# Attention operands of a hybrid layer turned by transposing transfers instead of on TensorE

## The chip, the cores and the metric

The kernel runs on one core of a Trainium2 chip. The metric is the device time of one execution in microseconds; below, "median" is the median of three runs. PE is TensorE, PEld its weight loads, DVE VectorE, ACT ScalarE, POOL GpSimd, SP SyncE. Transfers are issued from SP, POOL or ACT and run on the core's 16 DMA engines.

## What is computed

One decoder layer on 256 tokens of width 2048, in float32: a half-step SwiGLU feed-forward (width 5632), a mixer (chunked spatial gating beside a Mamba-2 scan) between one input and one output projection, cross attention of 4 heads of 512 into 256 memory tokens, a second half-step feed-forward, a final norm. The change touches the attention:

```python
def memory_cross_attention(hn, memn, w_q, w_kv, w_o):
    q = (hn @ w_q).reshape(bn, s, XA_HEADS, XA_HEADDIM)
    k, v = jnp.split(memn @ w_kv, 2, axis=-1)
    ...
    logits = jnp.einsum('bshd,bmhd->bhsm', q, k).astype(jnp.float32) * (XA_HEADDIM ** -0.5)
    probs = jax.nn.softmax(logits, axis=-1).astype(v.dtype)
    o = jnp.einsum('bhsm,bmhd->bshd', probs, v).reshape(bn, s, D_MODEL)
    return o @ w_o
```

## The kernel before

Precision is kept by splitting. Each float32 operand x becomes a high part (a rounded copy, type fp32r) and a low part (x minus the high part); a product is three matmuls, high by high, high by low and low by high. Activations are split once, weights as they stream in.

**A projection** (`proj_sum`) takes the weights in eight pieces of 256 rows by two blocks of 512 columns (1 MB). A piece is loaded by SP into one of three buffers (`wraw`), its high part is cast by ACT (`high`, L169), its low part subtracted by DVE (`low` through `split_op`, L177). There are three buffers for high and two for low parts. A plain piece (kind "C") takes 24 matmuls of 512 columns. A piece with sums (kind "S") combines blocks as in Strassen's scheme: three more DVE additions and a second split, but 21 matmuls. Eight PSUM banks are in use while a projection has S pieces ahead; four of them are combined after the last S piece (`mid`, `parts_of`), the others at the end (`evac`). The attention's projections are two for queries (heads 0 and 1, then 2 and 3), two for keys, two for values, each with eight pieces of which two have sums, in fourth and sixth place.

**The order of work.** PE runs in the order in which the program is written. Work beside the weights is put off with `later(fn, by)`: `step()` is called after each piece (or half piece) and runs the jobs that are due, counted in pieces; a job that needs a PSUM bank is held back while the S pieces run, unless it is marked `bankless`. On the other engines the framework's scheduler orders instructions when the program is built, within their dependencies and within the explicit orders that `behind` adds: casts and splits of weights (`last_cast`, `last_split`) keep their order, and `in_turn` puts the casts and splits of a source named "turned" into that order too.

**Temporaries** of 2 KB per partition (`half_k`, tag "t2k") share six buffers: partial results ("part"), copies ("halves"), turned operands ("turned"), probabilities ("probs"), sums of operands ("forms").

**How operands are turned.** PE needs activations with the features on the partitions. In the two feed-forwards the hidden activations go through DRAM (`Pieces.turn_later`, L481): ACT copies each 128 x 512 block so that the upper and lower 16 bits of its numbers lie apart ("halves", L485), POOL writes them to a DRAM tile ("planes", L487), and one piece later SP reads 256 columns at a time back with a transposing transfer ("turned", L491), which works on 16-bit elements. Four pieces later ACT and DVE split the turned block (L385, L386, or L471 to L477 for an S piece).

In the attention, queries and keys are turned on PE. `by_head` (L1034) collects a head's result and calls `operand_later`, which in `to_operand` makes four PE transposes (L77) per half into a PSUM bank one piece after the projection (L385 and L386 split from there). `attend` (from two pieces after the key projection) makes the logits, 24 matmuls per head, then maximum, exponentials and scaling (L1059 to L1068). `turn_probs`, 1.5 pieces later, transposes the probabilities on PE, and they are split at L992 and L993. `weigh` multiplies them with the values one and two pieces after the value projections.

Of the kernel before, what the change touches and what calls it, by code (L numbers as in the profile page):

```python
# [17 lines left out]
P = 128  # L18
# [29 lines left out]
def hybrid_layer(ctx: ExitStack, tc: tile.TileContext, x, xt, mem, memt, w_gu1, w_dn1, w_in, w_s, w_out,  # L48
# [30 lines left out]
    def later(fn, by=1, bankless=False):  # L79
        put_off.append((steps[0] + by, len(put_off), fn, bankless))  # L80
# [12 lines left out]
    def half_k(dtype, name):  # L93
        return tmp.tile([P, NC], dtype, name=name, tag="t2k")
# [267 lines left out]
        return r  # L362


    def in_turn(src, last, op):

        if not src.tensor.name.startswith("turned"):
            return op()
        with behind(last):
            ins = op()  # L370
        last[:] = [ins.ins]
        return ins

    def to_operand(srcs, dst, q, c0=None, of=None):
        of = q if of is None else of
        if isinstance(srcs, list):
            ps = side("tpose").rearrange("p (k s) -> p k s", k=2)
            for k in range(2):
                for t in range(NT):
                    transpose(out=ps[:, k, t * P:(t + 1) * P],  # L380
                              in_=srcs[t][:, (of + k) * P:(of + k + 1) * P], identity=ident)
        else:
            ps = srcs
        if c0 is None:
            hi = in_turn(ps, last_cast, lambda: nc.scalar.copy(out=dst[:, q:q + 2, :S], in_=ps))  # L385
            lo = in_turn(ps, last_split, lambda: nc.vector.tensor_tensor(  # L386
                out=dst[:, q:q + 2, S:], in0=ps, in1=dst[:, q:q + 2, :S].bitcast(F32), op=ALU.subtract))
        else:
            scs = [col[:, c0 + of + k:c0 + of + k + 1] for k in range(2)]
            for k in range(2):  # L390
                hi = nc.scalar.activation(dst[:, q + k, :S], ps[:, k, :], AF.Copy, scale=scs[k])
            for k in range(2):
                lo = nc.vector.scalar_tensor_tensor(out=dst[:, q + k, S:], in0=ps[:, k, :], scalar=scs[k],
                                                    in1=dst[:, q + k, :S].bitcast(F32),
                                                    op0=ALU.mult, op1=ALU.subtract)
        return hi.ins, lo.ins


    def operand_later(srcs, to, name, c0=None, by=1):
        def half(q):  # L400
            if q == 0:
                to.append(slot([P, KG, 2 * S], F32R, name))
            return to_operand(srcs, to[at], q, c0)

        at = len(to) + sum(1 for o in owed if o is to)
        owed.append(to)

        def first():
            owed.remove(to)
            assert len(to) == at  # L410
            half(0)
            later(lambda: half(2), by=0)

        later(first, by)

    owed = []


    class Pieces(dict):
        def __init__(self, kinds, name, donor=None):  # L420

            self.kinds, self.name, self.half, self.made, self.donor = kinds, name, None, {}, donor

        def add(self, srcs, q, c0):

# [31 lines left out]
        def sums(self, dst, ps, c0=None):  # L457
            in_sbuf = ps.tensor.name.startswith("turned")
            if not in_sbuf or c0 is not None:
                a = half_k(F32, "forms").rearrange("p (f s) -> p f s", f=4)  # L460
            if in_sbuf and c0 is None:
                a = ps
            elif c0 is None:
                nc.scalar.copy(out=a, in_=ps)
            else:
                for k in range(2):
                    nc.scalar.activation(a[:, 2 * k:2 * k + 2], ps[:, 2 * k:2 * k + 2], AF.Copy,
                                         scale=col[:, c0 + k:c0 + k + 1])

            b = half_k(F32, "forms").rearrange("p (f s) -> p f s", f=4)  # L470
            in_turn(a, last_split, lambda: nc.vector.tensor_tensor(  # L471
                out=b[:, 0:2], in0=a[:, 1:2].broadcast_to([P, 2, P]), in1=a[:, 0:4:3], op=ALU.subtract))
            nc.vector.tensor_tensor(out=b[:, 2], in0=a[:, 0], in1=b[:, 1], op=ALU.subtract)
            nc.vector.tensor_tensor(out=b[:, 3], in0=a[:, 2], in1=b[:, 2], op=ALU.subtract)
            for x, f0, f1 in ((a, 0, 4), (b, 4, 8)):
                hi = in_turn(x, last_cast, lambda: nc.scalar.copy(out=dst[:, 0, f0:f1], in_=x))
                lo = nc.vector.tensor_tensor(out=dst[:, 1, f0:f1], in0=x, in1=dst[:, 0, f0:f1].bitcast(F32),  # L477
                                             op=ALU.subtract)
            return hi.ins, lo.ins

        def turn_later(self, srcs, by):  # L481
            planes = dram.tile([S, 2, NC], U16, name="planes", tag="planes", bufs=2)
            for t in range(NT):
                halves = tmp.tile([P, 2 * NC], U16, name="halves", tag="t2k")
                nc.scalar.copy(out=halves.rearrange("p (b n) -> p b n", b=2),  # L485
                               in_=srcs[t].bitcast(U16).rearrange("p (n b) -> p b n", b=2))
                nc.gpsimd.dma_start(out=planes[t * P:(t + 1) * P].rearrange("p b n -> p (b n)"), in_=halves)  # L487
            for q in (0, 2):
                def fetch(q=q):
                    to = half_k(F32, "turned").rearrange("p (k s) -> p k s", k=KP)  # L490
                    nc.sync.dma_start(out=to.bitcast(U16).rearrange("p k s -> p (k s)").rearrange("p (k s) -> p k s", k=KP),  # L491
                                      in_=planes[:, :, q * P:(q + 2) * P].rearrange("s b n -> (s b) n"), transpose=True)
                    later(lambda: self.put(len(self), to, 0, None), by=by[1], bankless=True)
                later(fetch, by=by[0] + q / 4, bankless=True)

        def later(self, srcs, c0=None, by=1):
            for q in (0, 2):
# [530 lines left out]
    def by_head(to, name, scale=None):  # L1028
        got = {}

        def take(j, t, x):
            got[j, t] = x
            if scale is not None:
                nc.scalar.mul(x, x, scale[:, t:t + 1])  # L1034
            if t == 1:
                operand_later([got[j, 0], got[j, 1]], to, name, by=1 + j / 2)

        return take

# [10 lines left out]
    def attend(hd, kt):  # L1050
        lg = side("logits").rearrange("p (t m) -> p t m", t=NT)
        for t in range(NT):
            for i in range(4):
                qh, ql = qts[hd][:, i, t * P:(t + 1) * P], qts[hd][:, i, S + t * P:S + (t + 1) * P]
                matmul(lg[:, t, :], qh, kt[:, i, :S], start=(i == 0), stop=False)
                matmul(lg[:, t, :], qh, kt[:, i, S:])
                matmul(lg[:, t, :], ql, kt[:, i, :S], start=False, stop=(i == 3))
        mx = small.tile([P, NT], F32, name="mx")
        nc.vector.tensor_reduce(out=mx, in_=lg, axis=AX.X, op=ALU.max)  # L1059
        nc.vector.scalar_tensor_tensor(out=mx, in0=mx, scalar=-1.0, in1=lscale, op0=ALU.mult, op1=ALU.mult)  # L1060
        pr = half_k(F32, "probs").rearrange("p (t m) -> p t m", t=NT)
        sm = small.tile([P, NT], F32, name="sm")
        for t in range(NT):
            nc.scalar.activation(pr[:, t, :], lg[:, t, :], AF.Exp, bias=mx[:, t:t + 1], scale=lscale[:, t:t + 1],
                                 accum_out=sm[:, t:t + 1])
        nc.vector.reciprocal(out=sm, in_=sm)
        for t in range(NT):
            nc.vector.tensor_scalar(out=pr[:, t, :], in0=pr[:, t, :], scalar1=sm[:, t:t + 1], scalar2=None, op0=ALU.mult)  # L1068
        later(lambda: turn_probs(hd, pr), by=1.5)

    def turn_probs(hd, pr):
        tps = side("tpose").rearrange("p (m s) -> p m s", m=2)
        for m in range(2):
            for t in range(NT):
                transpose(out=tps[:, m, t * P:(t + 1) * P], in_=pr[:, t, m * P:(m + 1) * P], identity=ident)
        if hd % 2 == 0:
            pts.append(slot([P, 2, 2, 2 * S], F32R, "pts"))
        split_to(pts[hd // 2][:, hd % 2], tps)

    for hd in (0, 2):  # L1080
        heads(w_kv, mem_ts, MEM_KINDS, MEM_ORDER, hd * XD, by_head(kts, "kt", rstd_mem))
        for j in range(2):
            later(lambda hd=hd + j: attend(hd, kts[hd]), by=2 + j / 2)

    O_KINDS = "CCCSCSCC"
    ots = Pieces(O_KINDS, "ot")
# [100 lines left out]
```

## Time and profile before

| | |
|---|---|
| three runs | 2435.13, 2433.65, 2434.24 us; median 2434.24 |
| the profiled execution | 2435.73 us, span 2433.9 us |
| DMA | 503.86 MB, mean 207 GB/s |
| ScalarE casts of weights (L169, raw) | 787.2 us, 438 instructions |
| VectorE splits of weights (L177, lo from raw) | 944.8 us, 446 instructions |

How it is read: a row of the profile gives for an engine or a group of instructions the time in which it was busy; the chain of waits follows the execution back from its last instruction, at each step to what released it. Matmuls overlap in PE, so the length of one record is more than the time that it takes from PE; that time is read from the distance between starts, or from the lengths in the chain. A transfer has an issuing time on its queue and a time to landing.

### The profile page before, as it was taken

The page shows a single profiled execution, that of the slowest core. Times are in us where ns is not written, and L with a number is a line of the kernel's source. Part 1 is how long each engine was busy: PE and PEld are TensorE (multiplying, and loading weights), DVE is VectorE, ACT ScalarE, POOL GpSimd, SP SyncE. Part 2 cuts the span into 40 slices and gives each one's busy share as a digit, 9 for nine tenths or more (in the row PEclk, how much of TensorE's full clock was granted, in tenths as well). Part 3 has the DMA queues.
Part 4 walks back from the last instruction along what each step waited for, and adds up shares of the span by engine and source line. Part 5 has one row for each costly group of instructions (what it writes and reads, how often), then busy time and mean ns, then how long its engine had stood idle before and what let it go on. Part 6 is the DMA issues. An engine that isn't in the chain of part 4 may idle for free.

```text
span 2433.9 us, 29019 instructions
## 1 busy us (share of the span) xinstructions
PE 2420.0 (99%) x11189; PEld 2015.2 (83%) x11189; DVE 2033.6 (84%) x1936; ACT 1351.3 (56%) x1248; POOL 51.3 (2%) x104
## 2 busy tenths in 40 slices
PE   9999999999999999999999999999999999999998
PEld 7888888888888888788888888888888888888887
DVE  7999889999877777655698988778899988899997
ACT  6666445656546554435555655555566554556554
POOL 0000000000000000000000000000000000000000
PEclk9999999999999999999999999999999999999999
DMA  8768667777655555545566655555567776777774
GB/s 294 230 223 242 203 198 233 223 228 231 203 185 191 183 182 190 191 163 185 187 204 226 231 188 171 173 178 180 187 217 241 225 210 205 220 227 228 232 219 154
DMA packets 252714, 503.86 MB, mean 207 GB/s; under 512 B 62864, under 2 KB 66992, under 8 KB 251808
## 3 DMA queue, kind: packets, MB, share of 16 engines
q1 hardware_dynamic: 245696, 477.95, 61.7%
q0 software_dynamic: 6048, 23.02, 2.5%
q8 instruction: 87, 1.43, 0.2%
q10 hardware_dynamic: 832, 1.05, 0.1%
q14 instruction: 51, 0.42, 0.0%
HBM read 476.76 MB, written 13.66 MB: 201 GB/s over the span
## 4 chain that ended last, share of the span: by engine, by line
PE 95%; issue 2%; DMA 1%; DVE 0%; ACT 0%; SPq 0%; POOL 0%; POOLq 0%; DVEq 0%; ACTq 0%
PE acc L74 91%; PE tpose L77 1%; DMA raw<-in_w_gu 1%; PE yp L74 1%; PE o L74 0%; PE logits L74 0%; DMA h<-in_x 0%; PE mixed L74 0%; PE dt L74 0%; DVE sum L177 0%; PE scores L74 0%; PE yo L74 0%; PE st L74 0%; ACT hi L169 0%; DVE lo L177 0%
## 5 line engine op out<-in xcount | busy, mean ns | idle before, releaser
L177 DVE TENSOR_TENSOR lo<-raw,hi 128x2048 fp32r<-128x2048 f32 (+2 forms) x446 | 944.8, 2119 | 259.1 <-PE acc L74 197.5
L169 ACT CAST hi<-raw 128x2048 fp32r<-128x2048 f32 (+1 forms) x438 | 787.2, 1798 | 515.9 <-PE acc L74 441.9
L74 PE MATMUL acc<-hi,xp_ffn 128*128 128x512 f32 x1824 | 574.6, 390 | 0.0
L74 PEld LDWEIGHTS acc<-hi,xp_ffn 128*128 128x128 f32 x1824 | 342.8, 188 | 71.2
L169 ACT CAST hi<-sum 128x2048 fp32r<-128x2048 f32 x117 | 224.1, 1915 | 294.1 <-DVE sum L177 156.5
L74 PE MATMUL acc<-lo,xp_ffn 128*128 128x512 f32 x912 | 355.3, 390 | 2.0 <-DVE lo L177 2.0
L177 DVE TENSOR_TENSOR lo<-sum,hi 128x2048 fp32r<-128x2048 f32 x117 | 268.1, 2292 | 36.7 <-ACT hi L169 36.6
L74 PE MATMUL acc<-hi,hid 128*128 128x512 f32 x896 | 281.8, 389 | 0.0
L74 PE MATMUL acc<-hi,xt_mix 128*128 128x512 f32 x768 | 242.6, 393 | 0.0
L74 PEld LDWEIGHTS acc<-lo,xp_ffn 128*128 128x128 f32 x912 | 171.3, 188 | 38.6 <-DVE lo L177 3.2
L568 DVE TENSOR_TENSOR part<-acc,part 128x512 f32<-128x512 f32 x272 | 180.7, 686 | 22.1 <-PE acc L74 8.7
L74 PEld LDWEIGHTS acc<-hi,hid 128*128 128x128 f32 x896 | 168.2, 188 | 34.9
L74 PE MATMUL acc<-lo,hid 128*128 128x512 f32 x448 | 174.3, 389 | 0.0
L74 PEld LDWEIGHTS acc<-hi,xt_mix 128*128 128x128 f32 x768 | 144.2, 188 | 30.6 <-issue 1.0
L177 DVE TENSOR_TENSOR sum<-sum,raw 128x512 f32<-128x512 f32 x234 | 161.6, 691 | 6.2
L74 PE MATMUL acc<-lo,xt_mix 128*128 128x512 f32 x384 | 149.6, 390 | 0.0
L74 PE MATMUL acc<-hi,xp_ffn1s 128*128 128x512 f32 x466 | 148.6, 389 | 0.0
L74 PE MATMUL acc<-hi,xp_ffn2s 128*128 128x512 f32 x466 | 148.5, 389 | 0.0
L177 DVE TENSOR_TENSOR sum<-raw 128x1024 f32<-128x1024 f32 x117 | 142.5, 1218 | 0.3 <-DMA raw<-in_w_gu 0.3
L74 PE MATMUL acc<-xt_mix,hi 128*128 128x512 f32 x512 | 140.5, 396 | 0.0
L74 PE MATMUL acc<-hi,hids 128*128 128x512 f32 x392 | 125.2, 389 | 0.0
L74 PE MATMUL acc<-hi,memt 128*128 128x512 f32 x384 | 123.4, 392 | 0.0
(292 smaller groups left out, 3147.7 us busy)
## 6 DMA issues: line engine op xcount, KB each, us to landing
raw<-in_w_gu SPq DMA_DIRECT2D x286, 512.0 KB, 4.6
raw<-in_w_in SPq DMA_DIRECT2D x80, 1024.0 KB, 5.1
raw<-in_w_dn SPq DMA_DIRECT2D x60, 1024.0 KB, 5.2
raw<-in_w_gu SPq DMA_DIRECT2D x132, 256.0 KB, 4.9
raw<-in_w_kv SPq DMA_DIRECT2D x24, 1024.0 KB, 5.2
raw<-in_w_out SPq DMA_DIRECT2D x21, 1024.0 KB, 5.1
raw<-in_w_dn SPq DMA_DIRECT2D x28, 512.0 KB, 4.1
raw<-in_w_dn SPq DMA_DIRECT2D x56, 256.0 KB, 4.6
```

The costliest lines, as they stand in the source:

```text
L74: return pe(nc.tensor.matmul(out, lhsT=lhsT, rhs=rhs, start=start, stop=stop))
L77: return pe(nc.tensor.transpose(out=out, in_=in_, identity=identity))
L169: last_cast[:] = [nc.scalar.copy(out=t[:, :n], in_=x[:, :n]).ins]
L177: last_split[:] = [nc.vector.tensor_tensor(**kw).ins]
L568: nc.vector.tensor_tensor(out=out, in0=a, in1=b, op=op)
```

## The change

`turn_later` is taken apart into functions that any operand can use: `write_planes` (copies and writes), `read_turned` (the transposing read) and `turn_over`. Queries and keys go through them with `operand_turned`: copies and writes at the end of the projection, reads 1 and 1.5 pieces later for the first head and 1.25 and 1.75 for the second, splits 4 pieces after each read. The probabilities are copied and written in `attend`, read one piece later and split four pieces after that, from SBUF instead of PSUM. The logits are due 7 and 7.5 pieces after the key projection instead of 2 and 2.5.

```diff
+    def write_planes(srcs, n=NC):
+        planes = dram.tile([len(srcs) * P, 2, n], U16, name="planes", tag="planes", bufs=4)
+        for t, src in enumerate(srcs):
+            halves = tmp.tile([P, 2 * n], U16, name="halves", tag="t2k")
+            nc.scalar.copy(out=halves.rearrange("p (b n) -> p b n", b=2),
+                           in_=src.bitcast(U16).rearrange("p (n b) -> p b n", b=2))
+            nc.gpsimd.dma_start(out=planes[t * P:(t + 1) * P].rearrange("p b n -> p (b n)"), in_=halves)
+        return planes
+
+    def read_turned(to, planes, c0, n):
+        nc.sync.dma_start(out=to, in_=planes[:, :, c0:c0 + n].rearrange("s b n -> (s b) n"), transpose=True)
+
+    def turn_over(srcs, by, put):
+        planes = write_planes(srcs)
+
+        def fetch(q):
+            to = half_k(F32, "turned")
+            read_turned(to.bitcast(U16).rearrange("p (k s) -> p k s", k=KP), planes, q * P, KP * P)
+            later(lambda: put(to.rearrange("p (k s) -> p k s", k=KP), q), by=by[1], bankless=True)
+
+        for q in (0, 2):
+            later(lambda q=q: fetch(q), by=by[0] + q / 4, bankless=True)
+
-    def in_turn(src, last, op):
-
-        if not src.tensor.name.startswith("turned"):
+    def in_turn(src, last, op, c0=None):
+
+        if not src.tensor.name.startswith("turned") or c0 is not None and c0 < C_MIX:
             return op()
...
+    def operand_turned(srcs, to, name, c0=None, by=(1, 4)):
+        at = len(to) + sum(1 for o in owed if o is to)
+        owed.append(to)
+
+        def put(src, q):
+            if q == 0:
+                owed.remove(to)
+                assert len(to) == at
+                to.append(slot([P, KG, 2 * S], F32R, name))
+            to_operand(src, to[at], q, c0)
+
+        turn_over(srcs, by, put)
+
...
-        def turn_later(self, srcs, by):
-            planes = dram.tile([S, 2, NC], U16, name="planes", tag="planes", bufs=2)
...
+        def turn_later(self, srcs, by, c0=None, at=None):
+            if at is None:
+                at = self.due
+                self.due += 2
+            turn_over(srcs, by, lambda to, q: self.put(at + q // 2, to, q, c0))
...
-                operand_later([got[j, 0], got[j, 1]], to, name, by=1 + j / 2)
+                operand_turned([got[j, 0], got[j, 1]], to, name, by=(1 + j / 4, 4))
...
-        later(lambda: turn_probs(hd, pr), by=1.5)
-
-    def turn_probs(hd, pr):
-        tps = side("tpose").rearrange("p (m s) -> p m s", m=2)
-        for m in range(2):
-            for t in range(NT):
-                transpose(out=tps[:, m, t * P:(t + 1) * P], in_=pr[:, t, m * P:(m + 1) * P], identity=ident)
+        planes = write_planes([pr[:, t, :] for t in range(NT)], S)
+        later(lambda: turn_probs(hd, planes), by=1, bankless=True)
+
+    def turn_probs(hd, planes):
+        to = half_k(F32, "turned")
+        read_turned(to.bitcast(U16).rearrange("p (k s) -> p k s", k=KP), planes, 0, S)
+        later(lambda: split_probs(hd, to.rearrange("p (m s) -> p m s", m=2)), by=4, bankless=True)
+
+    def split_probs(hd, tps):
         if hd % 2 == 0:
             pts.append(slot([P, 2, 2, 2 * S], F32R, "pts"))
-        split_to(pts[hd // 2][:, hd % 2], tps)
+        to_operand(tps, pts[hd // 2][:, hd % 2], 0)
...
-            later(lambda hd=hd + j: attend(hd, kts[hd]), by=2 + j / 2)
+            later(lambda hd=hd + j: attend(hd, kts[hd]), by=7 + j / 2)
```

The parts left out pass the scale's column `c0` on to `in_turn` in `to_operand` and `Pieces.sums`, so that scaled casts and splits of a turned source would keep the order as well.

More of the change, by code (lines that the diff above doesn't have):

```diff
@@ L390, in to_operand @@
             for k in range(2):
-                hi = nc.scalar.activation(dst[:, q + k, :S], ps[:, k, :], AF.Copy, scale=scs[k])
+                hi = in_turn(ps, last_cast, lambda k=k: nc.scalar.activation(
+                    dst[:, q + k, :S], ps[:, k, :], AF.Copy, scale=scs[k]), c0)
             for k in range(2):
-                lo = nc.vector.scalar_tensor_tensor(out=dst[:, q + k, S:], in0=ps[:, k, :], scalar=scs[k],
-                                                    in1=dst[:, q + k, :S].bitcast(F32),
-                                                    op0=ALU.mult, op1=ALU.subtract)
+                lo = in_turn(ps, last_split, lambda k=k: nc.vector.scalar_tensor_tensor(
+                    out=dst[:, q + k, S:], in0=ps[:, k, :], scalar=scs[k], in1=dst[:, q + k, :S].bitcast(F32),
+                    op0=ALU.mult, op1=ALU.subtract), c0)
         return hi.ins, lo.ins
@@ L422, in __init__ @@
             self.kinds, self.name, self.half, self.made, self.donor = kinds, name, None, {}, donor
+            self.due = 0
         def add(self, srcs, q, c0):
@@ L466, in sums @@
                 for k in range(2):
-                    nc.scalar.activation(a[:, 2 * k:2 * k + 2], ps[:, 2 * k:2 * k + 2], AF.Copy,
-                                         scale=col[:, c0 + k:c0 + k + 1])
+                    in_turn(ps, last_cast, lambda k=k: nc.scalar.activation(
+                        a[:, 2 * k:2 * k + 2], ps[:, 2 * k:2 * k + 2], AF.Copy, scale=col[:, c0 + k:c0 + k + 1]), c0)
             b = half_k(F32, "forms").rearrange("p (f s) -> p f s", f=4)
-            in_turn(a, last_split, lambda: nc.vector.tensor_tensor(
-                out=b[:, 0:2], in0=a[:, 1:2].broadcast_to([P, 2, P]), in1=a[:, 0:4:3], op=ALU.subtract))
+            in_turn(ps, last_split, lambda: nc.vector.tensor_tensor(
+                out=b[:, 0:2], in0=a[:, 1:2].broadcast_to([P, 2, P]), in1=a[:, 0:4:3], op=ALU.subtract), c0)
             nc.vector.tensor_tensor(out=b[:, 2], in0=a[:, 0], in1=b[:, 1], op=ALU.subtract)
@@ L479, in sums @@
             return hi.ins, lo.ins
-        def turn_later(self, srcs, by):
-            planes = dram.tile([S, 2, NC], U16, name="planes", tag="planes", bufs=2)
-            for t in range(NT):
[L484 to L494, printed above, removed]
+        def turn_later(self, srcs, by, c0=None, at=None):
[3 more added lines that the diff above has]
+            turn_over(srcs, by, lambda to, q: self.put(at + q // 2, to, q, c0))
         def later(self, srcs, c0=None, by=1):
@@ L1068, in attend @@
             nc.vector.tensor_scalar(out=pr[:, t, :], in0=pr[:, t, :], scalar1=sm[:, t:t + 1], scalar2=None, op0=ALU.mult)
-        later(lambda: turn_probs(hd, pr), by=1.5)
-    def turn_probs(hd, pr):
-        tps = side("tpose").rearrange("p (m s) -> p m s", m=2)
-        for m in range(2):
-            for t in range(NT):
-                transpose(out=tps[:, m, t * P:(t + 1) * P], in_=pr[:, t, m * P:(m + 1) * P], identity=ident)
+        planes = write_planes([pr[:, t, :] for t in range(NT)], S)
[5 more added lines that the diff above has]
+    def split_probs(hd, tps):
         if hd % 2 == 0:
             pts.append(slot([P, 2, 2, 2 * S], F32R, "pts"))
-        split_to(pts[hd // 2][:, hd % 2], tps)
+        to_operand(tps, pts[hd // 2][:, hd % 2], 0)
     for hd in (0, 2):
```

## The prediction

> **What bounds the kernel now.** I read the page first, then the chain of waits inside the attention, then a table of windows, then the feed-forward groups, where the same kind of transfer already runs.
>
> ```profile
> span 2433.9 us, 29019 instructions
> PE 2420.0 (99%) x11189; PEld 2015.2 (83%) x11189; DVE 2033.6 (84%) x1936; ACT 1351.3 (56%) x1248; POOL 51.3 (2%) x104
> PE 95%; issue 2%; DMA 1%; DVE 0%; ACT 0%; SPq 0%; POOL 0%; POOLq 0%; DVEq 0%; ACTq 0%
> ```
>
> TensorE (PE) is busy 99% of the span and carries 95% of the chain that ends last. So an instruction taken off PE is time gained, as long as nothing makes PE wait instead. The chain between 1400 and 1600 us (second query projection, both key projections, start of the value projections) has 37 pieces; these are the ones of the second query projection and the first logits:
>
> ```profile
> by line: PE acc L74 90.0%; PE logits L74 5.7%; PE tpose L77 4.4%
> ...
> 1408.99 0.44 PE tpose L77 x4
> 1409.42 2.78 PE acc L74 x12
> 1412.20 0.87 PE tpose L77 x8
> ...
> 1415.82 0.44 PE tpose L77 x4
> 1416.26 36.78 PE acc L74 x162
> ...
> 1507.12 2.87 PE logits L74 x24
> ...
> 1533.32 0.87 PE tpose L77 x8
> ```
>
> The columns are start, length, what, how many instructions. Every piece is PE: nobody else is ever late here. 162 matmuls take 36.78 us, 0.227 us each, so a plain piece of weights (24 matmuls) is 5.45 us and a piece with sums (21) 4.77 us. The windows say the same; the first four are the second query, the two key and the first value projection, the next two are feed-forward groups, the last the 3 us in which two transposing transfers run:
>
> ```profile
> core 0: us, PE busy (x) PEld busy (x) DVE busy (x) ACT busy (x) POOL busy (x), PEclk, DMA share, GB/s
> 1405.00:1450.00 45.00, 45.00 (x208) 37.32 (x207) 39.79 (x44) 26.21 (x29) 0.30 (x2) 1.00 0.60 194
> 1450.00:1497.00 47.00, 47.00 (x217) 38.82 (x216) 39.96 (x37) 27.43 (x25) 0.00 (x0) 1.00 0.60 191
> 1497.00:1548.00 51.00, 51.00 (x263) 43.39 (x262) 38.77 (x41) 28.21 (x31) 0.00 (x0) 1.00 0.50 165
> 1548.00:1595.00 47.00, 47.00 (x243) 40.00 (x241) 36.14 (x39) 24.11 (x27) 0.00 (x0) 1.00 0.51 163
> 2100.00:2143.00 43.00, 43.00 (x192) 35.60 (x190) 39.43 (x34) 25.91 (x20) 1.08 (x2) 1.00 0.77 231
> 2143.00:2186.00 43.00, 43.00 (x191) 35.63 (x190) 39.55 (x33) 25.19 (x19) 1.08 (x2) 1.00 0.74 229
> 2145.00:2148.00 3.00, 3.00 (x15) 2.45 (x15) 3.00 (x2) 1.49 (x1) 0.00 (x0) 1.00 1.16 185
> ```
>
> PE has no idle time in any of them and the clock is full. VectorE (DVE) has 40 us of work in 47 in the attention, and 39.4 in 43 in a feed-forward group. T below is the step at which a projection ends; a step is one piece.
>
> **Removed: 80 transposes on PE.**
>
> ```profile
> L77 PE MATMUL tpose<-ident,part x64: 270/272/273, 1408.8 to 1554.8; 128*128 128x128 f32 x64
> L77 PE MATMUL tpose<-ident,probs x16: 272/272/273, 1533.2 to 1584.7; 128*128 128x128 f32 x16
> ```
>
> Queries and keys have 64, in each of four projections a group of 4, one of 8, one of 4; the probabilities have 16, in two groups of 8. By the chain a 4 takes 0.44 us and an 8 takes 0.87: 8 x 0.44 + 6 x 0.87 = 8.74 us, 0.109 each. All of it lies on the path, since PE never waits there: -8.74 us.
>
> The records last 272 ns, two and a half times that, because they overlap. The Trainium skill (TensorE: Matmul & The Clock Gate, Part 4: PE-mode transpose) puts a 128x128 transpose inside a kernel at about 275 ns; by that the sum would be 80 x 275 ns = 22 us. The trace agrees with it as the length of a record, not as what the transpose takes from PE.
>
> **Added: the way through DRAM.** Per operand two copies on ScalarE (ACT), two writes from GpSimd (POOL), two transposing reads from SyncE (SP); per head of probabilities 2, 2 and 1. In all 24 copies, 24 writes, 20 reads. The feed-forward groups show them:
>
> ```profile
> L485 ACT COPY halves<-part x44: 1036/1046/1051, 59.4 to 2304.7; 128x1024 uint16<-128x1024 uint16 x44
> L487 POOL DMA_DIRECT2D planes<-halves x44: 542/542/637, 60.7 to 2306.0; - x44
> L491 SPq DMA_TRANSPOSE turned<-planes x44: 1225/1303/3480, 64.1 to 2311.8; - x44
> planes<-halves POOLq DMA_DIRECT2D x44, 256.0 KB, 4.4
> turned<-planes SPq DMA_TRANSPOSE x44, 4.1
> SPq L491 <- DMA planes<-halves: 29.2, 23, 2.4
> ```
>
> ACT: 16 x 1.05 us, and 8 copies of half the size for which there is no row, between half and all of 1.05: 21 to 25 us. The first four windows hold 106 us of ACT in 190; with 25 more it is 131, about 69%. Cost 0; were ACT full, all of it would count. POOL: 24 x 0.54 = 13 us on an engine with 0.3 us of work there. Cost 0.
>
> SP: 20 x 1.3 = 26 us, and each read waits for its writes, with the weight loads queued behind it. In a feed-forward group the wait is 1.3 us (29.2 over 23) and the two reads 2.6, so loads stand still 3.9 us; here, with two operands, up to 1.3 + 4 x 1.3 = 6.5 us at each of four ends of a projection. Loads at a feed-forward group's end stand still without any loss on PE, with DVE fuller (39.4 of 43) than here. I take 0; the other end is in the rivals.
>
> The DMA engines: in the 3 us of two reads they are full (share 1.16) and bring only 185 GB/s. The Trainium skill (DMA: Bandwidth & Descriptors, Specifications) says that transfers in pieces under 512 B fall below line rate, which speaks against this change; the trace agrees, 185 GB/s at a full share against 229 at 0.74 in the window of 43 us around it. Four reads need 6 us of the engines per projection, and the share there is 0.5 to 0.6; 6 of 47 us more is 0.13, the four writes less than that, which ends near the 0.77 of the feed-forward groups.
>
> **Changed in place: the splits.** They read SBUF, not PSUM.
>
> ```profile
> L385 ACT CAST kt<-tpose x8: 566/584/594, 1497.8 to 1555.1; 128x512 fp32r<-128x512 f32 x8
> L386 DVE TENSOR_TENSOR kt<-tpose,kt x8: 680/688/692, 1498.4 to 1556.2; 128x512 fp32r<-128x512 f32 x8
> L385 ACT CAST hid<-turned x28: 610/613/616, 74.7 to 2278.4; 128x512 fp32r<-128x512 f32 x28
> L386 DVE TENSOR_TENSOR hid<-turned,hid x28: 683/685/685, 77.9 to 2281.7; 128x512 fp32r<-128x512 f32 x28
> ```
>
> Twenty of each: ACT +0.6 us, DVE nothing. They also no longer need a PSUM bank. Cost 0.
>
> **Moved: the logits, from T+2 to T+7.** Each head's 24 matmuls (2.87 us), maximum, exponentials and scaling go past five pieces on PE, and past their splits on ACT and DVE; new behind them are the copies, writes and read of the probabilities. The work is the same. What goes is 5.7 us of PE time that stood ahead of the first piece with sums, in which DVE could catch up; the key splits and the maxima leave the same place. The second query projection has no logits ahead of its sums and shows PE 45.00 of 45.00. Cost 0. Ready keys: in a feed-forward group the way from the first copy to the last split is
>
> ```profile
> L485 ACT COPY halves<-part x2: 1039/1042/1046, 2135.6 to 2138.8; 128x1024 uint16<-128x1024 uint16 x2
> L386 DVE TENSOR_TENSOR hid<-turned,hid x2: 685/685/685, 2154.0 to 2157.3; 128x512 fp32r<-128x512 f32 x2
> ```
>
> 2158.0 - 2135.6 = 22.4 us with the same due steps for its two halves. Seven pieces, two with sums, are 5 x 5.45 + 2 x 4.77 = 36.8 us: 14 us to spare. Probabilities are split at T+12 and used at T+17. Cost 0. Queries are needed later still.
>
> **The rest of the diff** executes what stood. Only the input of the first feed-forward is both turned and scaled, its c0 is below C_MIX, and so it is still not put behind the last cast or split; the pieces of the feed-forwards get the same numbers; four buffers for the planes instead of two can only lift a wait. Cost 0.
>
> **Sum.** -8.74 us. The profiled execution took 2435.73 us, 1.83 outside its span; it would be 2427.0. The median of before is 2434.24, so I forecast 2425.5 us. 0.2%, 4.9 us, is about what a measurement of this kernel can tell from no change.
>
> **Rivals.**
> 1. Weights late. The 6.5 us in which loads stand still are not hidden by the one piece (5.45 us) that is split ahead: 1.05 us lost at each of four projections, 4.2 in all: 2429.7. Against it: the feed-forward groups, and that in the attention casts wait for PE to free a buffer and not for loads:
>
> ```profile
> ACT hi L169 <- PE acc L74: 39.2, 16, 4.2
> ```
>
> That is 2.5 us to spare for each of 16 casts. For it: twice as many reads in one place. Without any split ahead, 6.5 - 2.5 = 4.0 us each would be lost, 16 in all.
> 2. Slower: the keys come late at the logits of heads 2 and 3. The pool for temporaries has six buffers. At the end of the second key projection four hold its result, one a head's probabilities, and copies have one left. A copy holds its buffer for 1.05 + 0.54 + 4.4 = 6.0 us. If all eight copies there (four of probabilities, four of keys) go through one buffer, the way is 48 + 1.3 + 4.1 + 0.6 + 0.7 = 54.7 us against 36.8: PE waits 17.9 us, with all later matmuls behind it, and the time is 2425.5 + 17.9 = 2443.4. It decides from 8.7 us late, when more than six of the eight go one behind the other. Against it: each pair of copied results frees two buffers at once.
> 3. The record's length is the price: 80 x 272 ns = 21.8 us off, 2412.5. The chain speaks against it: eight transposes in 0.87 us. The page on TensorE above would have it so.
>
> **Chances.** Forecast 0.80, weights late 0.12, slower 0.06, record's length 0.02. Runs of before spread by 0.7 us to either side and the sum's terms are measured, so below I go to 2424.0. Above, the range takes in the weights being late with 1.3 us more: 2431.0. That leaves out 0.08 and the tails. Faster by over 0.2% (under 2429.4): 0.80 + 0.02 and the lighter part of rival 1, 0.02: 0.84. Same: 0.10. Slower: 0.06.
>
> **What would show it.** PE busy near 2411 us with 80 fewer matmuls, no tpose fed by part or probs, chain in the attention all PE. ACT up by 21 to 25 us, DVE unchanged, POOL +13, 64 transposing reads. Rival 1 would show as PE or PEld waiting for DVE lo with ACT hi waiting for a load; rival 2 as PE logits waiting for the split of kt. Wrong I would be if PE's idle time rose by 4 us or more, wherever.

## The result and the profile after

The changed kernel takes 2447.68 us (median of six runs, 2445.65 to 2451.57) against 2434.57 us for the kernel before in the same series: the ratio is 1.0055 [1.0044, 1.0065]. It is slower by 0.55%, where 2425.5 us was forecast. Two executions, one of the kernel before and one of run 2 below, ran at a much lower clock (4510.15 and 3108.87 us); they are left out of the medians and of every comparison. The profiled execution took 2448.37 us. Its page:

```profile
span 2446.7 us, 29000 instructions
PE 2419.4 (99%) x11109; PEld 2010.2 (82%) x11109; DVE 2033.2 (83%) x1936; ACT 1371.0 (56%) x1272; POOL 66.3 (3%) x128
PE 88%; issue 8%; DMA 1%; ACT 1%; DVE 1%; POOL 1%; SPq 0%; POOLq 0%; ACTq 0%; DVEq 0%
```

PE has 80 matmuls fewer, as it should, and yet is busy for as long as before (in part because the half clock found below lengthens its records); its share of the chain has fallen from 95% to 88%. The windows of the attention (second query, first key, second key, first value projection; columns as in the prediction) show where:

```profile
1405.00:1445.00 40.00, 36.90 (x161) 29.60 (x160) 32.65 (x36) 26.45 (x33) 5.13 (x6) 1.00 0.76 220
1445.00:1495.00 50.00, 45.67 (x189) 36.86 (x188) 37.99 (x38) 28.16 (x27) 2.24 (x4) 0.93 0.76 226
1495.00:1540.00 45.00, 44.34 (x203) 36.66 (x202) 35.81 (x29) 28.49 (x24) 2.17 (x4) 1.00 0.77 240
1540.00:1595.00 55.00, 47.93 (x212) 38.52 (x211) 36.57 (x40) 32.52 (x38) 4.34 (x8) 0.94 0.70 192
```

Where PE was busy for every microsecond of before, it now idles 190.00 - 174.84 = 15.2 us, and in two of the windows the granted clock (the share of its full clock that PE was given) is below 1. The waits between 1400 and 1600 us say for whom (the last row is the queue of SP's transfers):

```profile
PEld acc L74 <- DVE lo L177: 19.2, 10, 3.4
PE acc L74 <- DVE lo L177: 15.0, 9, 3.1
ACT hi L169 <- DMA raw<-in_w_kv: 6.4, 2, 3.4
ACT hi L169 <- DMA raw<-in_w_q: 4.1, 1, 4.1
ACT kt L408 <- DMA turned<-planes: 6.5, 4, 3.6
ACT halves L369 <- DMA planes<-halves: 3.0, 2, 2.1
SPq L375 <- DMA planes<-halves: 24.1, 7, 6.7
```

PE and its weight loads wait for low parts of weights. Behind that ACT waits for loads of weights, for which it had no wait in these 200 us before, for turned blocks, and for a buffer that a write still holds; and SP waits 24.1 us in seven reads for the writes to land, 3.4 us each, not the 1.3 us of a feed-forward group.

Most of it falls on one kind of piece: the second piece with sums of a projection, with 13.0 of the 15.1 us of pauses in PE's rows. The first key projection shows it best. In the kernel before, the low part of that piece's sums is ready just in time (start, length, what; the number in brackets is idle time):

```profile
1476.99 2.29 DVE L177 TENSOR_TENSOR lo<-sum,hi 128x2048 fp32r<-128x2048 f32 x1 [0.39 <-ACT hi L169]
1478.53 0.39 PE L74 MATMUL acc<-hi,memts 128*128 128x512 f32 x1
1479.34 0.19 PEld L74 LDWEIGHTS acc<-lo,memts 128*128 128x128 f32 x1 [0.17 <-DVE lo L177]
```

It ends at 1476.99 + 2.29 = 1479.28, and PEld, which had stood waiting for it for 0.17 us, takes it up at 1479.34. The wait cost PE nothing, but nothing was left to spare either. In the same way the second query projection has 0.8 us to spare there, the second key and the first value projection 1.3 us each. So "PE has no idle time" was true of before and said nothing of how near it was to having some. These are the loads on SP around that piece, before and after the change, and then what ACT, DVE and PE did after it:

```profile
1452.49 0.38 SPq L140 DMA_DIRECT2D raw<-in_w_kv  x1
1458.39 0.38 SPq L151 DMA_DIRECT2D raw<-in_w_kv  x1
```

```profile
1453.19 0.38 SPq L140 DMA_DIRECT2D raw<-in_w_kv  x1
1454.85 9.87 SPq L375 DMA_TRANSPOSE turned<-planes  x3
1464.83 0.60 SPq L151 DMA_DIRECT2D raw<-in_w_kv  x1
1465.53 1.24 SPq L375 DMA_TRANSPOSE turned<-planes  x1
1466.82 1.04 SPq L154 DMA_DIRECT2D raw<-in_w_kv  x2
```

```profile
1472.76 1.48 ACT L169 CAST hi<-raw 128x1536 fp32r<-128x1536 f32 x1 [3.40 <-DMA raw<-in_w_kv]
1477.36 0.39 PE L74 MATMUL acc<-hi,memts 128*128 128x512 f32 x1
1480.39 0.50 PE L74 MATMUL acc<-lo,memts 128*128 128x512 f32 x1 [2.65 <-DVE lo L177]
1480.69 2.29 DVE L177 TENSOR_TENSOR lo<-sum,hi 128x2048 fp32r<-128x2048 f32 x1 [0.35 <-ACT hi L169]
1483.04 0.79 PE L74 MATMUL acc<-lo,memts 128*128 128x512 f32 x1 [1.68 <-DVE lo L177]
```

L151 and L154 are the loads of the second piece with sums. In the kernel before SP issues nothing between 1452.9 and 1458.4 either, 5.5 us: there it waits until DVE has freed a buffer. Now it is 11.3 us, 1453.6 to 1464.8: three reads stand there with their waits, 9.87 us, and the fourth stands in the middle of the next load. ACT waits 3.40 us for that load, DVE's low part of the sums ends 5.6 us after PE has begun the piece (0.8 us after in the kernel before: 1479.28 and 1478.53), and PE stops twice in it, for 2.65 and 1.68 us.

Then comes something that no row of before shows:

```profile
1477.00:1483.50 6.50, 2.17 (x8) 1.23 (x7) 6.08 (x6) 4.74 (x5) 0.00 (x0) 0.88 0.29 83
1483.50:1488.50 5.00, 5.00 (x13) 3.84 (x13) 2.89 (x3) 1.76 (x1) 0.00 (x0) 0.50 0.55 177
1585.50:1591.00 5.50, 5.50 (x13) 4.33 (x14) 3.23 (x3) 2.10 (x2) 0.00 (x0) 0.50 0.60 202
```

After these pauses, and again after those of the first value projection, PE works for 5 to 6 us at half clock: the 13 matmuls of a window take 0.4 us each instead of 0.227. That is 2.5 and 2.75 us more. 15.2 us of idle time and 5.25 us of half clock make 20.4 us; the 23.0 us found below are more. Counted from start to start, the pauses take 16.9 us beyond a matmul's 0.227 us, because a record of 0.39 us covers part of each pause, and the matmuls that start over 0.33 us apart take 6.6 us beyond it: 23.5 us.

### The profile page after: what moved, and what is told of

Its sections match the earlier page's. It is cut to its first block, busy times and chain, and to the rows that moved or that the text cites. A ratio compares the mean times of both kernels' runs of the same rounds, so it can differ in the third digit from the quotient of the medians.

```text
span 2446.7 us, 29000 instructions
## 1 busy us (share of the span) xinstructions
PE 2419.4 (99%) x11109; PEld 2010.2 (82%) x11109; DVE 2033.2 (83%) x1936; ACT 1371.0 (56%) x1272; POOL 66.3 (3%) x128
## 4 chain that ended last, share of the span: by engine, by line
PE 88%; issue 8%; DMA 1%; ACT 1%; DVE 1%; POOL 1%; SPq 0%; POOLq 0%; ACTq 0%; DVEq 0%
PE acc L74 85%; PE tpose L77 1%; PE yp L74 1%; DMA raw<-in_w_gu 0%; PE o L74 0%; ACT hi L169 0%; POOL planes L371 0%; PE mixed L74 0%; DVE lo L177 0%; PE logits L74 0%; DMA turned<-planes 0%; DMA planes<-halves 0%; DVE sum L177 0%; PE dt L74 0%; PE scores L74 0%
## 5 line engine op out<-in xcount | busy, mean ns | idle before, releaser
L177 DVE TENSOR_TENSOR lo<-raw,hi 128x2048 fp32r<-128x2048 f32 (+2 forms) x446 | 944.6, 2119 | 265.6 <-PE acc L74 183.7
L177 DVE TENSOR_TENSOR lo<-sum,hi 128x2048 fp32r<-128x2048 f32 x117 | 268.1, 2291 | 41.0 <-ACT hi L169 40.8
L177 DVE TENSOR_TENSOR sum<-sum,raw 128x512 f32<-128x512 f32 x234 | 161.5, 690 | 6.3
L177 DVE TENSOR_TENSOR sum<-raw 128x1024 f32<-128x1024 f32 x117 | 142.4, 1217 | 1.6 <-DMA raw<-in_w_kv 0.7
```

The costliest lines, as they stand in the source:

```text
L177: last_split[:] = [nc.vector.tensor_tensor(**kw).ins]
```

## The experiments

Times are medians; the interval is that of the ratio to the kernel before, whose median in the four series was 2434.60 (first four runs), 2434.79 (next four), 2434.49 (two) and 2434.89 us (last four). "Second S piece" is short for the second piece with sums.

**1. The logits alone.** The kernel before with `by=7 + j / 2` for `attend`.

> The kernel before with one edit: the logits due 7 and 7.5 pieces after the key projection instead of 2 and 2.5; everything is still turned on PE. Logits theory (5.7 us of PE work no longer stands ahead of the pieces with sums, so VectorE is late there): at least half of the 22 us of idle PE appears, 2445 us or more. Queue theory (the reads stand on SP right ahead of the load of each projection's second piece with sums and wait there for the plane writes) and engines theory (the transposing reads fill the DMA engines): no change, 2434.6 within 2 us, PE busy in every window of the attention.

2435.22 us, 1.0002 [0.9993, 1.0012], PE busy in every microsecond of the four windows. Moving the logits costs nothing and gains nothing that this run can show, as the prediction had it.

**2. The reads behind the load.** The changed kernel, with the reads of the attention put on SP behind the load of the second S piece, and split one piece after they are read:

```diff
-        nc.sync.dma_start(out=to, in_=planes[:, :, c0:c0 + n].rearrange("s b n -> (s b) n"), transpose=True)
+        with behind(order):   # order: the load traced last
+            nc.sync.dma_start(out=to, in_=planes[:, :, c0:c0 + n].rearrange("s b n -> (s b) n"), transpose=True)
...
-                operand_turned([got[j, 0], got[j, 1]], to, name, by=(1 + j / 4, 4))
+                operand_turned([got[j, 0], got[j, 1]], to, name, by=(4, 1))
```

Loads are written two pieces ahead here, and the probabilities are read after 3 pieces and split 2 later. Loads written two pieces ahead were not run by themselves.

> The changed kernel with the same copies, writes and reads, but the attention's reads ordered on SP behind the load of the projection's second piece with sums (loads are traced two pieces ahead in the attention so that this order can be stated); keys still split before the logits at 7 and 7.5 pieces. Queue theory: the loads are on time, SP's waits for plane writes fall from 24 us to under 8, PE's idle time goes, 2426 to 2430 us. Engines theory: the same 20 reads in the same projections cost the same, 2445 within 3 us.

2438.74 us, 1.0017 [1.0008, 1.0027]. SP's wait for the writes fell from 24.1 to 7.9 us, as intended, but only 8.9 us came back, a time between the two theories. So the queue of SP is a cause and not the only one. The trace showed the turned casts (`qt`, `kt`) waiting on ACT for their reads, ahead of the casts of the second S piece.

**3. Plain reads.** In the attention each transposing read is replaced by two plain ones of half the bytes, at the same place and with the same waits, and the copies don't part the halves; the operands are not turned.

> The changed kernel with the attention's 20 transposing reads replaced by 40 plain reads of the same bytes at the same place on SP, waiting for the same writes; the attention's operands are therefore not turned (that part of the computation is changed). Queue theory with the wait as the price: SP still waits over 20 us and most of the loss stays, 2440 us or more. Engines theory, or SP's own 1.3 us per transposing read as the price: 2426 to 2432 us.

2438.60 us, 1.0021 [1.0011, 1.0031]: 9.1 us back, between the two theories. SP still waits 29.9 us in eight reads, so the waits are not the transposition's; a pair of plain reads issues in 2 x 0.46 us instead of 1.25. What more the 9.1 us are was not traced.

**4. The probabilities alone.** The kernel before with only the probabilities going through DRAM, logits at 2.

> The kernel before with the probabilities alone through DRAM (4 reads, 16 PE transposes fewer); queries and keys on PE, logits 2 and 2.5 pieces after the keys. The reads stand on SP ahead of plain pieces, one at a time. Queue theory: no loss and the 1.7 us of the two groups of 8 gained, 2432.8 within 1 us. Engines theory: a fifth of the reads, a fifth of the loss, 2434.6 - 1.7 + 4.4 = 2437.

2432.19 us, 0.9989 [0.9979, 0.9998], 2.4 us less; 16 x 0.109 = 1.7 us are the transposes, and the rest is within the interval. SP's row is the telling one:

```profile
SPq L375 <- DMA planes<-halves: 20.5, 5, 8.9
```

SP stands still for 20.5 us here, nearly as long as in the changed kernel, and PE doesn't wait once. Its reads stand ahead of plain pieces, one at a time, and the load behind the first goes out 12.2 us after the load ahead of it (1506.84 to 1519.02), as in the kernel before (1508.75 to 1520.95), where it waits for a buffer. So here the wait of SP has no price of its own; what counts is whether the load behind it goes out later.

**5 and 6. Late casts; later logits.** Run 2 with the casts of turned queries and keys one piece later (`by=(4, 2)`, logits at 8), so that they stand on ACT behind those of the second S piece; then with the logits at 9 as well.

> The kernel of the reads behind the load of the second piece with sums, with one thing more: the casts of the turned queries and keys are given out one step later, so that they stand on ScalarE behind the casts of that piece too, and the logits one step later (8, 8.5). Theory 'casts' (what was left of the loss there, 2439.0 against the 2425.8 that 8.7 us less would give, are turned casts that wait on ScalarE for their reads ahead of the casts of the second piece with sums): the gaps of PE at that piece of the second query and of the two keys go (2.1, 2.0 and 0.7 us), that of the first value, which has the same cause and the halves of the probabilities besides, shrinks from 8.5 to 2 to 4 us; 2428 to 2432, faster than before. Theory 'engines' (the transposing reads themselves slow the weights' loads): the reads are all there still, 2437 to 2440.

> The same with the logits one step later again (9, 9.5), so that the halves of the probabilities of the first two heads are no longer copied on ScalarE between the two halves of the evacuation of the second key and the casts of a piece with sums. Theory 'casts': the gap of the first value goes as well, 2425 to 2428. Theory 'engines': as the run before, 2437 to 2440. If logits at 9 hold the probabilities up until the first output needs them: PE waits for pts in the second value projection, several us.

2426.57 us, 0.9964 [0.9951, 0.9976], and 2425.55 us, 0.9962 [0.9949, 0.9976]. The first is faster than either theory had it. The two can't be told apart; both beat the kernel before and the changed one, and the second is within 0.1 us of the forecast, closer than its own runs agree (2424.78 to 2427.64). Its page, its windows and SP at the place shown above:

```profile
PE 2410.6 (99%) x11109; PEld 2007.3 (83%) x11109; DVE 2032.1 (84%) x1936; ACT 1370.4 (57%) x1272; POOL 66.2 (3%) x128
PE 95%; issue 3%; DMA 1%; DVE 1%; ACT 0%; SPq 0%; POOL 0%; POOLq 0%; DVEq 0%; ACTq 0%
```

```profile
1405.00:1445.00 40.00, 40.00 (x178) 33.15 (x177) 34.69 (x35) 27.26 (x31) 5.12 (x6) 1.00 0.84 248
1445.00:1495.00 50.00, 49.59 (x219) 40.73 (x219) 41.39 (x42) 35.25 (x36) 3.32 (x6) 1.00 0.79 243
1495.00:1540.00 45.00, 45.00 (x210) 37.68 (x209) 36.43 (x30) 29.12 (x25) 3.25 (x6) 1.00 0.84 257
1540.00:1595.00 55.00, 55.00 (x283) 47.06 (x283) 45.19 (x53) 34.25 (x41) 2.15 (x4) 1.00 0.75 219
```

```profile
1454.96 0.38 SPq L153 DMA_DIRECT2D raw<-in_w_kv  x1
1455.38 1.34 SPq L156 DMA_DIRECT2D raw<-in_w_kv  x2
1457.15 6.09 SPq L382 DMA_TRANSPOSE turned<-planes  x4
```

The load of the second S piece of the first key projection goes out 8.1 us after the last start of `hi,xp_xa`, the end of the queries, against 14.2 in the changed kernel and 8.5 in the kernel before (1446.9, 1450.6 and 1449.9 in the rows further down); the four reads follow within 6.09 us. PE idles 0.41 us in 190. All the copies, writes and transposing reads are still there, and the DMA engines' share is higher than in the changed kernel (0.75 to 0.84 against 0.70 to 0.77), so the engines' load by itself is not what cost.

With the three kernels the price can be set out. The attention, from the first matmul of the queries to the first of the output projection (first and last start of each group, in the kernel before, the changed kernel and run 6):

```profile
L74 PE MATMUL acc<-hi,xp_xa x192: 389/389/478, 1362.0 to 1449.9; 128*128 128x512 f32 x192
L74 PE MATMUL acc<-hi,ot x192: 389/389/477, 1643.6 to 1735.3; 128*128 128x512 f32 x192
```

```profile
L74 PE MATMUL acc<-hi,xp_xa x192: 388/389/478, 1360.7 to 1450.6; 128*128 128x512 f32 x192
L74 PE MATMUL acc<-hi,ot x192: 389/389/477, 1656.7 to 1748.4; 128*128 128x512 f32 x192
```

```profile
L74 PE MATMUL acc<-hi,xp_xa x192: 389/389/478, 1360.9 to 1446.9; 128*128 128x512 f32 x192
L74 PE MATMUL acc<-hi,ot x192: 389/389/477, 1633.9 to 1725.6; 128*128 128x512 f32 x192
```

That is 281.6, 296.0 and 273.0 us: the transposes are worth 8.6 us, and the changed kernel loses 23.0.

**7. Queries and keys alone.** The changed kernel with the probabilities transposed on PE as before.

> The change for queries and keys alone: the probabilities are transposed on PE as before, logits five pieces later. 7.0 us of the 8.7 are saved (32 transposes of 40 ... 64 of 80). Theory 'queue' (four reads and their waits ahead of the load of the second piece with sums): the gaps at the second query and the first and second key as in the changed kernel (3.8, 7.6, 0.9), at the first value only the share of the second key's four reads, 4 to 8 of 11; 2441 to 2447, clearly slower than before. Theory 'probabilities' (what is lost at the first value comes from their round trip): that gap goes, 2436 to 2439.

2441.77 us, 1.0030 [1.0019, 1.0042]. The loss of the first key projection is much as in the changed kernel (3.5 us idle instead of 4.3, and a clock of 0.93 in the second window), that of the first value projection mostly gone (1.9 us idle in the fourth instead of 7.1). So probabilities, which cost nothing by themselves, seem to cost where their copies and reads come on top of those of the keys. But the first window, with no probabilities near, also has 1.2 us idle instead of 3.1; so some 2 us between two single profiles may not be the edit's.

**8. Late casts alone.** The changed kernel with `by=(1 + j / 4, 5)` and the logits at 8; the reads stay ahead of the load.

> The changed kernel with the casts of the turned queries and keys one step later (behind the casts of the second piece with sums on ScalarE), the logits at 8, 8.5; the reads stay on SP where they are, ahead of that piece's load. Theory 'queue': the load is late whatever ScalarE does, so at most 2 to 5 us come back, 2442 to 2447. Theory 'casts' (ScalarE's order alone is the price): 2428 to 2434.

2436.75 us, 1.0009 [1.0000, 1.0018]: 10.9 us back, between the two theories again. ACT now waits longer for loads of weights than in the changed kernel (12.7 us in three casts and 8.4 in one), and PE loses less.

**9. Copies and writes alone.** The kernel before with `write_planes` called for queries and keys and nothing read back; PE transposes as before.

> The kernel before, with queries and keys copied into halves on ScalarE and written to DRAM as in the change, but never read back: PE transposes them as before, so nothing is saved and no read stands on SP. Theory 'reads' (what costs is the reads that wait on SP and the turned casts that wait for them on ScalarE): 2434 to 2436, no gap of PE at the second piece with sums. Theory 'copies' (the 16 copies of some 1.3 us each are themselves enough to make the casts of that piece late, since it has hardly a us to spare): 2437 to 2442, with gaps at the same pieces as in the changed kernel.

2441.39 us, 1.0026 [1.0015, 1.0036]: 6.9 us slower without a single read, so the reads are not the only cause. The waits of ACT between 1400 and 1600 us:

```profile
ACT halves L369 <- DMA planes<-halves: 9.4, 4, 4.0
ACT junk L353 <- DMA planes<-halves: 5.2, 1, 5.2
ACT forms L476 <- DMA planes<-halves: 3.0, 1, 3.0
```

17.6 us, all for one of the six temporaries that a write still holds, on the engine that has to cast the weights. The changed kernel has 3.0 us of such waits. For in run 9 the results stay in their temporaries until PE has turned them, beside their copies, and the six buffers are scarcer. PE's pauses also lie elsewhere: 4.8 of 5.8 us at the first piece with sums of the second query and the first key projection, where the changed kernel has none. The two longest:

```profile
1426.71 0.50 PE L74 MATMUL acc<-lo,xp_xas 128*128 128x512 f32 x1 [2.64 <-DVE lo L177]
1474.29 0.50 PE L74 MATMUL acc<-lo,memts 128*128 128x512 f32 x1 [1.47 <-DVE lo L177]
```

So this run shows that copies with their writes can cost by themselves, not that 6.9 of the changed kernel's 23.0 us are theirs.

**10 to 13. A seventh temporary.** `bufs=7`, in the changed kernel twice (10 and 11), in run 9 (12) and in the kernel before (13). Room for it comes from the tile of zeros of the first idle matmuls, which lies in a temporary in run 10, and from run 11 on where x lies later:

```diff
-    tmp = ctx.enter_context(tc.tile_pool(name="tmp", bufs=6))
+    tmp = ctx.enter_context(tc.tile_pool(name="tmp", bufs=7))
...
-    idle = const.tile([P, S], F32, name="idle")
+    idle = h[3][:, 0, :S]
```

> The changed kernel with seven temporaries instead of six (the tile of zeros that fed the idle matmuls lies in one of them for its time). Theory 'temporaries' (halves, turned pieces and probabilities wait for each other's buffers, so that reads come late): part of the loss comes back, 2436 to 2443. Theory 'order' (the reads wait for the writes to land, and the load and the casts of the second piece with sums stand behind them in the order of the program): 2445 to 2450, as the changed kernel.

> The changed kernel with seven temporaries again, but the tile of zeros for the first idle matmuls now lies where x will lie later, so that the start isn't late (in the run before, the first idle matmul began at 9.62 us instead of 1.28). Theory 'temporaries' (the sixth buffer missing is most of the loss): the attention, from the first matmul of the queries to the first of the output projection, takes some 281 us as in the run before, instead of 296.0; 2431 to 2434. Theory 'start' (that run's gain came from somewhere at its start): 2440 or more.

> The kernel before with copies and writes of queries and keys that nobody reads, and seven temporaries. Theory 'buffers' (copies and other work of ScalarE wait in line for a buffer that a write still holds: 17.6 us of such waits in the run with six): most of its 6.9 us comes back, 2434 to 2437. Theory 'copies' (the copies' own 16 x 1.3 us are the price): 2439 to 2442.

> The kernel before with seven temporaries and nothing else: the control. PE had no idle time in the attention there, so both theories expect no difference, 2433.5 to 2435.5. If it is faster by over 2 us, the seventh temporary's gain is not one of the change.

Run 10: 2437.81 us, 1.0014 [1.0004, 1.0023]. Run 11: 2436.24 us, 1.0007 [0.9998, 1.0016], so 11.4 us of the loss come back; less than the 13 to 17 expected. Run 12: 2436.70 us, 1.0009 [1.0000, 1.0018]; 4.7 of the 6.9 us come back, and of the 17.6 us of ACT's waits for a write this is left:

```profile
ACT junk L353 <- DMA planes<-halves: 1.1, 1, 1.1
```

Run 13: 2435.31 us, 1.0002 [0.9993, 1.0011]: without the change the seventh buffer does nothing that can be measured. So most of what copies cost in run 9 is waiting for a buffer; what is left in run 12, 1.8 us (0.0 to 4.4), is the most that their own time takes there. Which waits the seventh buffer shortens in the changed kernel was not traced: its PE pauses are 7.1 us in run 11 instead of 15.1, all still in second S pieces.

**14. All of it.** Run 6 with seven temporaries.

> The fastest version so far (reads behind the load, late casts, logits at 9, 2425.55) with seven temporaries. If the three causes are one and the same lateness of the second piece with sums, nothing is left to win: 2424.5 to 2426, PE without a gap over 0.5 us in the attention. If temporaries cost something of their own, 2421 to 2424.

2426.88 us, 0.9969 [0.9957, 0.9981]: no faster than run 6. Where the reads and the casts stand behind the second S piece, six buffers are enough.

**Together.** Of the changed kernel's 22.1 us above run 6, the order on SP gives back 8.9, the order on ACT 10.9, and both together all of it: these two nearly add up. Plain reads give back 9.1 and a seventh buffer 11.4. All four would be 40 us for 22, so these last two shorten delays that the two orders shorten too. That all four are steps on one path (load, cast, sums, low part of the second S piece), which has 0 to 1.3 us to spare in the four projections read above, is how the traces read; what each adds at each place was not measured.

## Why the prediction was wrong

- **-8.74 us for 80 transposes: right.** 8.6 us between the kernel before and run 6. The record's length as the price (rival 3) is out.
- **The logits at T+7, cost 0: right** (run 1). **The splits, and the rest of the diff, cost 0:** DVE is at 2033.2 against 2033.6 us, and run 6, at the forecast's time, leaves no room for more. ACT grew by 19.7 us, a little under the 21 to 25; POOL by 15.0 us for 13.
- **"Loads at a feed-forward group's end stand still without any loss on PE, with DVE fuller (39.4 of 43) than here. I take 0": this step failed.** It took the cover from another place, where two reads come together and not four, and measured it by how full DVE was on average. What counts is how long before PE needs it the next weights are split. In the first key projection the four reads and their waits took 9.87 + 1.24 = 11.1 us of SP, not 6.5, because SP waited 3.4 us per waiting read and up to 6.7, not 1.3; and the load behind them was that of a second S piece, which went out 5.7 us later than before (14.2 instead of 8.5 us after the queries). With the reads behind that load and the turned casts behind that piece's casts the time is the forecast's (run 6, 2425.55 us). Why the feed-forward groups stand their two reads so well was not tried; their waits are shorter and half as many reads come at once.
- **"ACT: ... Cost 0; were ACT full, all of it would count": this step failed too.** ACT isn't full (131 us of 190 was the estimate; 115.6 in 190 were measured, of a stretched attention), and yet 10.9 us come back when the turned casts stand one piece later on ACT and the reads stay where they are (run 8), and copies with their writes can cost 6.9 us by themselves (run 9, at other pieces). What counts is which weight cast stands behind a copy or cast that has to wait, not the share of busy time; the changed kernel's ACT waits 6.5 us for turned blocks of the keys alone.
- **Rival 1 was right in kind and far too small.** PE and PEld wait for DVE's low parts, and ACT for loads, as it said. It priced this at 4.2 us, 16 at most; it was 23.0. Its cushion of 2.5 us was a mean over 16 casts, and the piece that decides has 0 to 1.3 us; and the half clock after the pauses, 5.25 us, was in no sum.
- **Rival 2 did not happen.** PE never waits for keys at the logits. But the six temporaries that it named did cost, at another place: PE waits for low parts of weights, and a seventh gives 11.4 us back (run 11).
- The profile gave a sign of it. The row "1479.34 ... [0.17 <-DVE lo L177]" of the kernel before is a wait at the very piece, although PE has no idle time there.

## What to carry to other kernels

That an engine is busy all the time does not tell how much delay its suppliers can stand: find, in each stretch that an edit touches, the instruction whose operand is ready last, and read the time between the two from the timeline. When transfers, waits or casts are added to a queue, see in the order of that queue which load or cast stands behind them, and put them behind the piece with the least to spare; here the same work cost 22 us ahead of it and nothing behind it. Work that holds a shared buffer until a write lands can also stop an engine that has other work to do: in run 9 ACT stood 17.6 us for such buffers.

## What the runs showed of the hardware

The granted clock of PE fell to 0.50 for 3 to 6 us after some short pauses. In run 2 a single pause of over a microsecond was enough, with another of 0.37 us some 3 us ahead of it (PE's records, then the window behind it):

```profile
1563.47 0.50 PE L74 MATMUL acc<-hi,memt 128*128 128x512 f32 x1
1565.80 0.62 PE L74 MATMUL acc<-lo,memt 128*128 128x512 f32 x1 [1.83 <-DVE lo L179]
```

```profile
1566.00:1569.20 3.20, 3.20 (x9) 2.45 (x8) 3.20 (x6) 2.54 (x3) 0.00 (x0) 0.50 0.93 273
```

The pause was 1.83 us. In the changed kernel's second query projection two pauses in one piece, 1.5 and 1.9 us from start to start beyond a matmul's time, left the clock at full:

```profile
1436.00:1441.00 5.00, 5.00 (x22) 4.16 (x23) 5.00 (x7) 3.74 (x3) 0.00 (x0) 1.00 0.56 176
```

So the length of a single pause doesn't decide, and what does stays open. The Trainium skill (TensorE: Matmul & The Clock Gate, Why this matters for your kernels) advises against pauses of PE over about 3 us because the clock then falls back to half; the fall agrees with the rows here, the length does not: 1.83 us were enough once.
